# Placing the weight sums, the last run's row splits and the four-ahead row splits in a hybrid attention kernel

## The chip, the cores and the metric

The kernel runs on 1 core of one Trainium2 chip. The metric is the device time of one execution in microseconds (us), as the median of the runs given. The core has five engines with a queue each: TensorE (PE in the profile, with its weight loads as PEld), VectorE (DVE), ScalarE (ACT), GpSimd (POOL) and SyncE (SP), which here only issues DMAs. An engine takes its instructions in the order in which the program writes them to its queue; engines wait for one another, and for DMAs, through semaphores.

## The reference, cut to what matters

With DEPTH = 1 only the first layer runs, the one with the neighbourhood mixer. For x of 2048 tokens by 1024 columns, in float32:

```
h = rmsnorm(x, norm_0)
q, k, v, gate = split(h @ w_in_0, 4)               # 1024 x 4096
o = neighbourhood_attention(q, k, v, rpb_0)        # 16 heads of 64, 8 x 16 window on a 32 x 64 grid
x = x + (o * silu(gate)) @ w_out_0                 # 1024 x 1024
out = rmsnorm(x, norm_f)
```

Every matmul of the projections is done as three: an operand t is split into a high part h (ACT copies t to the rounding type fp32r) and a low part l = t - h (DVE), and the product is h·h + h·l + l·h. Part of the products are done by Strassen's scheme with seven block products in place of eight; for it sums and differences of blocks (called T1 to T4 on one side and S1 to S4 on the other) are formed and split too.

## The kernel before, in words

The program is written out by hand: Python code calls the engines in the order in which each queue is to work, and small closures are put into "slots" between groups of matmuls. Three parts matter here.

**Stage two** (`stage_two`) works on the second half of the tokens. First it forms the values v, as two groups of columns u = 0 and u = 1. `pair(u, ts, *do)` issues the 24 matmuls of each token tile in `ts` in four quarters (`values_of`, line L562) and calls `do[0]` to `do[3]` behind the quarters. Group 0 goes through four pairs of tiles, group 1 through eight single tiles 12, 13, 14, 15, 8, 9, 10, 11. In the slots stand:

- `lw`: loads of the weights of v by SP (L533); `w`: their splits, ACT L542 and DVE L545;
- `v`: the finished tile is taken from PSUM by ACT (L394) and stored by SP (L397);
- `block`, `t123`, `t4`, `form`, `t1`: sums and splits (ACT L520, DVE L521) of the token side for the seven products that follow;
- `out_rows(k)`: four loads of w_out rows by SP (L890), for k = 0 to 3; `out_sum(k, f)`: for T1, T3, T2, T4 in turn the difference of two of these rows on DVE (L897), its split (ACT L520 into `oh`, DVE L521 into `ol`) and two stores to DRAM by SP (L901), where the last stage fetches them;
- `ahead(i)`: loads, sums (DVE L427) and splits (ACT L420, DVE L421) of the weights for the seven products.

Then `run()` issues the seven products (L438) unit by unit in the order 1, 6, 2, 7, 5, 4, 3. Products 1 and 2 share a PSUM bank: `keep` (ACT L446) copies product 1 out before product 2 may be added to it, and `add` (DVE L451) does the like for 6 and 7.

**Attention** goes in 32 runs of (head pair, row block). `turns` transposes the probabilities on PE (L1136) and copies them from PSUM by ACT and DVE (L1112, three copies each); `values` multiplies them with v (L1158). Between them PE works on the `scores` (L1051) of the next run and on slices of other matmuls. Behind the last run there is no next one, so nothing lies between its transposes and its `values`.

**The output rows by seven products** (`rows_by_seven`) end the kernel: five pairs of output tiles, 35 products of 12 matmuls (L1439), of which the first 21 belong to pairs 0, 1 and 2 in an order written by hand (products 1 of the three pairs, products 2 of the three, and then mixed: places 16 to 20, counted from 0, are (1,3), (2,7), (2,5), (2,4), (2,3)), and 14 to pairs 3 and 4. `form_rows(m, P)` splits the operand of product P of pair m (ACT L1413, DVE L1414), `sum_rows` forms S1 to S4 (DVE L1420), `load_rows_of` fetches the blocks A11 to A22 (SP L1408). A table `todo` says behind which product each of these is issued. Behind a product, ACT or DVE take the result: L1444 for product 1, DVE L1449 and a sum on POOL (L1452, L1456) for 6 and 7, DVE L1236 (`add_rows`) for the rest; `finish` scales the finished rows (DVE L1279) some time later. Product 3 of a pair is added to the bank of product 5, so it waits until L1236 has read product 5.

The seven products' operands of the w_out side come back from DRAM through `land` (L1383). The splits of product 1 of pairs 0 to 2 stand ahead of `turns` of the last run, those of product 2 ahead of its `values`.

Of the kernel before, what the change touches and what calls it, by code (L numbers as in the profile page):

```python
# [32 lines left out]
PLAIN = 6  # L33
# [38 lines left out]
def build(ctx, tc, x, xr, xt, wg, rpb, last, w_out, n0, nf, masks, out):  # L72
# [728 lines left out]
    def stage_two():  # L801
        x12, x11, x21 = L2["x12"], L2["x11"], L2["x21"]
        x22 = [xp([128, 512], F32, "land") for _ in range(4)]
        sixth = sixths()
        for k in range(4):
            load_x(2, "x22", k, x22[k])
        slots = {"T2": [(mp, 512)] * 8,
                 "T3": [(sp, 512)] * 2 + sixth[:5] + [(lp, 512)],
                 "T4": [(vh, 512)] * 4 + [(mp, 512)] * 2 + [sixth[5], (qp, 512)]}

        def also(n, i):
            if n == 0:
                if i == 0:
                    load_ahead()
                    load_e(0, 0, xp)[0]()
                elif i == 1:
                    load_e(0, 0, xp)[1]()
                    load_masks()
                elif i == 2:
                    for f in load_e(order[1][0], 0, homes=accs):  # L820
                        f()
                if i in (1, 2, 3, 4):
                    consume(1)
                if i == 5:
                    consume(2)
                if i in (4, 5):
                    bias(0, 0, i - 4)
                if i == 3:
                    load_k(0, 0)()
                    load_q(0, 0)()  # L830

        ahead, run = seven_products(units_two, 2, X2, also)

        def pair(u, ts, *do):
            for b in range(4):
                values_of(X2, u, ts, (2 * b, 2 * b + 1))
                if b < len(do):
                    do[b]()

        def both(*fs):  # L840
            return lambda: [f() for f in fs]

        def block(f, x, *ks):
            def g():
                if f not in X2:
                    X2[f] = [(xs([128, 512], F32R, "h"), xs([128, 512], F32R, "l")) for _ in range(4)]
                for k in ks:
                    normed(f, 3, k, x[k])
# [12 lines left out]
        def t123(*ks):  # L861
            def g():
                for k in ks:
                    a, b, c = x11[k], x12[k], x22[k]
                    nc.vector.tensor_tensor(c, c, b, OP.subtract)
                    nc.vector.tensor_tensor(b, b, a, OP.subtract)
                    nc.vector.tensor_tensor(a, a, c, OP.add)
            return g

        def t4(*ks):  # L870
            def g():
                for k in ks:
# [12 lines left out]

        def out_rows(k):
            def g():
                for q, (r_, c_) in quarters.items():
                    OW[q] = kp([128, 960], F32, "ow")[:, :512] if r_ else ep([128, 512], F32, "ow")
                    nc.sync.dma_start(OW[q], w_out[(4 * r_ + k) * 128:(4 * r_ + k + 1) * 128, c_ * 512:c_ * 512 + 512])  # L890
            return g

        def out_sum(k, f):
            def g():
                a, b = {"T1": ("B12", "B11"), "T3": ("B22", "B12"), "T2": ("B22", "B11"), "T4": ("B21", "B22")}[f]
                o = OW[{"T1": "B11", "T3": "B12", "T2": "B22", "T4": "B21"}[f]]
                nc.vector.tensor_tensor(o, OW[a], OW[b], OP.subtract)  # L897
                h, l = ev([128, 512], F32R, "oh"), ev([128, 512], F32R, "ol")
                split_to(h, l, o, None)
                for i, s in enumerate((h, l)):  # L900
                    store(("ow", f, k, i), 5, lambda i=i, s=s: nc.sync.dma_start(wod[f][:, k, i], s.bitcast(F32)))  # L901
            return g

        def t1(*ks):
            def g():
                for k in ks:
                    split_to(*X2["B12"][k], x12[k], None)
                X2["T1"] = X2["B12"]
            return g

        pair(0, (8, 9), both(w(0, 3), lambda: spread_rstd(3)), both(lw(1, 0), block("B12", x12, 0, 1)),
             both(block("B12", x12, 2, 3), out_rows(0)), block("B22", x22, 0, 1))
        pair(0, (10, 11), both(v(0, 8, 9), block("B22", x22, 2, 3)), t123(0), t123(1), both(lw(1, 1), out_sum(0, "T1")))
        pair(0, (12, 13), both(v(0, 10, 11), out_sum(0, "T3")), t123(2), t123(3), both(t4(0, 1, 2, 3), lw(1, 2)))
        pair(0, (14, 15), both(v(0, 12, 13), w(1, 0), out_sum(0, "T2")), both(w(1, 1), lw(1, 3)), both(w(1, 2), out_sum(0, "T4")),
             both(w(1, 3), out_rows(1)))
        pair(1, (12,), v(0, 14, 15), form("T2", x11, 0), form("T2", x11, 1), out_sum(1, "T1"))
        pair(1, (13,), both(v(1, 12), form("T2", x11, 2)), form("T2", x11, 3), out_sum(1, "T3"), out_sum(1, "T2"))
        pair(1, (14,), both(v(1, 13), form("T3", x22, 0)), form("T3", x22, 1), out_sum(1, "T4"), out_rows(2))
        pair(1, (15,), both(v(1, 14), lambda: ahead(-9, -1)), form("T3", x22, 2), form("T3", x22, 3), out_sum(2, "T1"))  # L920
        pair(1, (8,), both(v(1, 15), lambda: ahead(-8, -1)), both(t1(0), out_sum(2, "T3")), t1(1), both(lambda: ahead(-7, -1), out_sum(2, "T2")))
        pair(1, (9,), both(v(1, 8), t1(2)), both(t1(3), out_sum(2, "T4")), both(lambda: ahead(-6, -1), out_rows(3)), form("T4", x21, 0))
        pair(1, (10,), both(v(1, 9), form("T4", x21, 1)), form("T4", x21, 2), both(form("T4", x21, 3), out_sum(3, "T1")), out_sum(3, "T3"))
        pair(1, (11,), both(v(1, 10), lambda: ahead(-5)), both(lambda: ahead(-4), out_sum(3, "T2")), both(lambda: ahead(-3), lambda: ahead(-2)),
             both(lambda: ahead(-1), v(1, 11), out_sum(3, "T4")))
        for k in range(4):
            hh[k, 2], hl[k, 2] = X2["B11"][k]
            hh[k, 3], hl[k, 3] = X2["B12"][k]
            hh[4 + k, 2], hl[4 + k, 2] = X2["B21"][k]
            hh[4 + k, 3], hl[4 + k, 3] = X2["B22"][k]  # L930
        run()
# [535 lines left out]
    def rows_by_seven():  # L1467
# [8 lines left out]
        def on(i, f, *a):  # L1476
            todo.setdefault(i, []).append((f, a))
# [11 lines left out]
            on(i, load_rest_of, m, j, k)  # L1489
        for m in range(E, len(PAIRS)):  # L1490
            s = seq.index((m, 1))
            for d, f in ((-7, "A21"), (-7, "A22"), (-6, "A11"), (-4, "A12")):
                on(s + d, load_rows_of, m, f)
            for d, f in ((-4, "S1"), (-4, "S2"), (-2, "S3"), (-1, "S4")):
                on(s + d, sum_rows, m, f)
            for d, j, k in ((-2, 0, 1), (-2, 0, 0), (-1, 1, 0), (0, 1, 1)):
                on(s + d, load_rest_of, m, j, k)
        for i, s in enumerate(seq):
            if i >= 2 * E:
                on(i - (LEAD if i < seq.index((E, 1)) else 3), form_rows, *s)  # L1500
        for f in ("A21", "A22"):
            load_rows_of(1, f, vh)
        for m in range(E):
            load_rest_of(m, 0, 0)
        land_T4()
        for i, (m, P) in enumerate(seq):
            rows_product(m, P)
            for d in sorted(todo):
# [77 lines left out]
    for m in range(cycles + 1):  # L1586
# [41 lines left out]
        if m == cycles:  # L1628
# [79 lines left out]
```

## Time and profile before

| | |
|---|---|
| times of the runs | 1059.3 us median of 3 (1059.07 to 1060.69) |
| the profiled execution's own time | 1060.0 us |
| its span, first to last instruction | 1058.2 us |
| mean granted TensorE clock | 0.995 |
| HBM traffic | 145.24 MB read, 58.72 MB written |
| slices of the span with PE at 9 tenths or more | 38 of 40 |

The profiled execution is one more run of the same program. A timeline row gives the start and the length of an instruction, its engine, its line and what it writes and reads, and in square brackets how long the engine had been idle before it and what ended that. The length of a matmul (0.39 us for 512 columns) is longer than the distance at which two can follow each other, since they overlap in the array. A row of SP is the issue of a DMA, not the transfer.

### The profile page before, as it was taken

The page shows a single profiled execution, that of the slowest core. Times are in us where ns is not written, and L with a number is a line of the kernel's source. Part 1 is how long each engine was busy: PE and PEld are TensorE (multiplying, and loading weights), DVE is VectorE, ACT ScalarE, POOL GpSimd, SP SyncE. Part 2 cuts the span into 40 slices and gives each one's busy share as a digit, 9 for nine tenths or more (in the row PEclk, how much of TensorE's full clock was granted, in tenths as well). Part 3 has the DMA queues.
Part 4 walks back from the last instruction along what each step waited for, and adds up shares of the span by engine and source line. Part 5 has one row for each costly group of instructions (what it writes and reads, how often), then busy time and mean ns, then how long its engine had stood idle before and what let it go on. Part 6 is the DMA issues. An engine that isn't in the chain of part 4 may idle for free.

```text
span 1058.2 us, 20319 instructions
## 1 busy us (share of the span) xinstructions
PE 1040.5 (98%) x7256; PEld 850.9 (80%) x7256; DVE 743.7 (70%) x1601; ACT 557.9 (53%) x1305; POOL 279.2 (26%) x357
## 2 busy tenths in 40 slices
PE   9999999999999999999999999999999999989997
PEld 6888888887888877888888788888888788878876
DVE  5376657778897857655554766677687797776986
ACT  7545323344344344332333477778888777663433
POOL 0000231322311000000000476755656424221331
PEclk9999999999999999999999999999999999999999
DMA  9633544443636587533244777788877599898452
GB/s 313 224 100 102 143 149 125 130 149 107 185 126 201 158 264 252 163 108 110 98 142 143 223 245 223 229 230 288 250 237 235 170 298 316 253 370 313 137 171 80
DMA packets 133213, 205.30 MB, mean 194 GB/s; under 512 B 12216, under 2 KB 56504, under 8 KB 133112
## 3 DMA queue, kind: packets, MB, share of 16 engines
q1 hardware_dynamic: 132680, 203.61, 60.6%
q8 instruction: 57, 0.93, 0.4%
q14 instruction: 44, 0.36, 0.1%
q10 hardware_dynamic: 432, 0.40, 0.1%
HBM read 145.24 MB, written 58.72 MB: 193 GB/s over the span
## 4 chain that ended last, share of the span: by engine, by line
PE 55%; DMA 2%; DVE 1%; ACT 1%; issue 1%; SPq 0%; DVEq 0%; ACTq 0%
PE pp L438 16%; PE py L1439 9%; PE s L1051 8%; PE o L1158 7%; PE ph L1136 4%; PE pp L384 2%; PE pp L386 2%; PE pp L382 2%; PE po L1360 2%; PE po L1362 2%; PE po L1364 2%; DMA t<-wodT 1%; DMA raw<-ogd 1%; DMA em<-in_last_dram 0%; DVE x L1059 0%
## 5 line engine op out<-in xcount | busy, mean ns | idle before, releaser
L438 PE MATMUL pp<-h,f 128*128 128x512 f32 x672 | 217.8, 389 | 2.8 <-ACT p L446 2.8
L1065 ACT ACTIVATE x<-x,st 128x360 f32<-128x360 f32 (+5 forms) x256 | 151.2, 592 | 24.7 <-DVE st L1059 24.7
L438 PEld LDWEIGHTS pp<-h,f 128*128 128x128 f32 x672 | 126.0, 188 | 29.5 <-ACT p L446 3.2
L438 PE MATMUL pp<-t,f 128*128 128x512 f32 x558 | 141.8, 389 | 0.1
L1079 POOL TENSOR_SCALAR x<-x,st 128x480 f32<-128x480 f32 (+5 forms) x192 | 114.4, 613 | 94.0 <-DVE st L1070 91.8
L438 PE MATMUL pp<-l,f 128*128 128x512 f32 x336 | 130.7, 389 | 0.0
L458 POOL TENSOR_TENSOR tmp<-tmp,rb 128x512 f32<-128x512 f32 x36 | 58.4, 1622 | 270.7 <-DVE tmp L456 235.3
L1059 DVE CUSTOM_DVE_ANT_0 x<-s,em 128x360 f32<-128x360 f32 (+5 forms) x256 | 123.0, 535 | 0.4 <-PE s L1051 0.4
L438 PEld LDWEIGHTS pp<-t,f 128*128 128x128 f32 x558 | 104.6, 188 | 22.5 <-DVE u L451 0.9
L1019 POOL TENSOR_TENSOR em<-e,mk 128x264 f32<-128x264 f32 (+3 forms) x64 | 50.8, 825 | 265.3 <-PE pp L438 251.8
L421 DVE TENSOR_TENSOR f<-raw,f 128x512 fp32r<-128x512 f32 x105 | 76.5, 729 | 37.5 <-ACT f L420 37.5
L1158 PEld LDWEIGHTS o<-pta,vt 120*64 120x64 f32 (+2 forms) x1792 | 82.7, 140 | 16.6 <-DVE st L1059 13.6
L1051 PE MATMUL s<-kt,q 64*128 64x480 f32 (+5 forms) x512 | 95.4, 487 | 0.1
L562 PE MATMUL pv<-wh,h 128*128 128x512 f32 x256 | 89.3, 394 | 2.0 <-ACT wh L542 2.0
L1158 PE MATMUL o<-pta,vt 120*64 120x128 f32 (+5 forms) x1792 | 87.4, 256 | 2.7 <-ACT pta L1112 2.4
L562 PE MATMUL pv<-wl,h 128*128 128x512 f32 x256 | 89.0, 393 | 0.3 <-DVE wl L545 0.3
L562 PE MATMUL pv<-wh,l 128*128 128x512 f32 x256 | 88.6, 391 | 0.0
L1051 PEld LDWEIGHTS s<-kt,q 64*128 64x128 f32 x512 | 64.7, 186 | 16.5 <-DVE pta L1112 2.3
L420 ACT ACTIVATE f<-raw 128x512 fp32r<-128x512 f32 x105 | 63.7, 624 | 26.2 <-PE pp L438 10.4
L1112 DVE COPY pta<-ph 120x512 f32<-120x512 f32 (+5 forms) x96 | 56.9, 639 | 23.9 <-PE ph L1136 23.7
L438 PEld LDWEIGHTS pp<-l,f 128*128 128x128 f32 x336 | 63.1, 188 | 13.1
L1112 ACT ACTIVATE pta<-ph 120x512 f32<-120x512 f32 (+5 forms) x96 | 49.5, 556 | 34.0 <-PE ph L1136 33.3
(186 smaller groups left out, 1861.4 us busy)
## 6 DMA issues: line engine op xcount, KB each, us to landing
raw<-in_wg_dram SPq DMA_DIRECT2D x124, 256.0 KB, 4.7
row<-in_xr_dram SPq DMA_DIRECT2D x32, 256.0 KB, 4.5
vd<-v SPq DMA_DIRECT2D x32, 256.0 KB, 3.0
sgd<-sg SPq DMA_DIRECT2D x32, 256.0 KB, 2.4
q<-qd SPq DMA_DIRECT2D x32, 256.0 KB, 5.6
sgt<-sgd SPq DMA_DIRECT2D x32, 256.0 KB, 6.3
xr<-in_x_dram SPq DMA_DIRECT2D x32, 256.0 KB, 5.2
ogd<-og SPq DMA_DIRECT2D x32, 256.0 KB, 4.0
```

Of the source, the lines that this page charges most:

```text
L420: nc.scalar.activation(t[:, 0], src, AF.Copy)
L421: nc.vector.tensor_tensor(t[:, 1], src, t[:, 0].bitcast(F32), OP.subtract)
L438: nc.tensor.matmul(B[n, P], t[:, int(m == 2), c], x[k][int(m == 1)], start=P in (1, 6, 5) and k == 0 and m == 0, stop=k == 3 and m == 2, s ...
L458: nc.gpsimd.tensor_tensor(tmp, tmp, rb[c], OP.mult)
L562: nc.tensor.matmul(ps[t], a[:, o], b, start=k == 0 and m == 0, stop=k == NK - 1 and m == 2)
L1051: nc.tensor.matmul(pst[s], qt[a, qs], kt[a, :r1 - r0, c0:c1].rearrange("p r (s c) -> p s r c", c=8), start=True, stop=True)
L1059: nc.vector.tensor_tensor_reduce(X[i, C][s], pst[s], EM[p, ROW_TYPE[T], COL_TYPE[C], s], -1.0, 1e38, OP.add, OP.min, st[:, o:o + 1])
L1065: nc.scalar.activation(X[i, C][s], X[i, C][s], AF.Exp, bias=st[:, o:o + 1], scale=-1.0, accum_out=st[:, 4 + o:5 + o])
L1079: nc.gpsimd.tensor_scalar(X[i, C][s], X[i, C][s], st[:, o:o + 1], 1.0, op0=OP.mult, op1=OP.mult)
L1112: (nc.vector.tensor_copy if h else lambda o, i_: nc.scalar.activation(o, i_, AF.Copy))(t[:k, h, b * 512:b * 512 + w], banks_[b, h][:k, :w])
L1158: nc.tensor.matmul(to.rearrange("d (h q) -> d h q", q=64) if nq > 64 else to, vt[:k, strip, s * 64:s * 64 + 64], t[:k, h, at:at + 64] if n ...
L1439: nc.tensor.matmul(B[m, P], t[:, a, c], b, start=P in (1, 6, 5) and k == 0 and i == 0, stop=k == 3 and i == 2, skip_group_check=True)
```

## The change

Three edits, all of them to the order in which things are issued; no operation is added or taken away.

1. In `stage_two`, `out_sum` is cut in two: `out_sum` does only the difference, `out_split` the split and the stores. In the list of pairs a sum now stands one slot ahead of its split, and the loads `out_rows(1)`, `(2)`, `(3)` and the sums are moved to other slots. For k = 3 the last split stands in tile 10's last slot, and tile 11's slots hold none.
2. The splits of product 1 of pairs 0 to 2 are issued behind the last run's `turns`, and those of product 2 behind its `values`, at the head of `rows_by_seven`.
3. In `rows_by_seven` the splits of pairs 3 and 4 are issued four products ahead in place of three, their S1, S3 and loads one to three products earlier.

```diff
                 o = OW[{"T1": "B11", "T3": "B12", "T2": "B22", "T4": "B21"}[f]]
                 nc.vector.tensor_tensor(o, OW[a], OW[b], OP.subtract)
+            return g
+
+        def out_split(k, f):
+            def g():
+                o = OW[{"T1": "B11", "T3": "B12", "T2": "B22", "T4": "B21"}[f]]
                 h, l = ev([128, 512], F32R, "oh"), ev([128, 512], F32R, "ol")
                 split_to(h, l, o, None)
...
+        def o(k, *fs):
+            return [(out_sum if f[0] == "+" else out_split)(k, "T" + f[-1]) for f in fs]
+
...
-        pair(0, (10, 11), both(v(0, 8, 9), block("B22", x22, 2, 3)), t123(0), t123(1), both(lw(1, 1), out_sum(0, "T1")))
-        pair(0, (12, 13), both(v(0, 10, 11), out_sum(0, "T3")), t123(2), t123(3), both(t4(0, 1, 2, 3), lw(1, 2)))
-        pair(0, (14, 15), both(v(0, 12, 13), w(1, 0), out_sum(0, "T2")), both(w(1, 1), lw(1, 3)), both(w(1, 2), out_sum(0, "T4")),
-             both(w(1, 3), out_rows(1)))
...
-        pair(1, (10,), both(v(1, 9), form("T4", x21, 1)), form("T4", x21, 2), both(form("T4", x21, 3), out_sum(3, "T1")), out_sum(3, "T3"))
-        pair(1, (11,), both(v(1, 10), lambda: ahead(-5)), both(lambda: ahead(-4), out_sum(3, "T2")), both(lambda: ahead(-3), lambda: ahead(-2)),
-             both(lambda: ahead(-1), v(1, 11), out_sum(3, "T4")))
+        pair(0, (10, 11), both(v(0, 8, 9), block("B22", x22, 2, 3)), t123(0), t123(1), both(lw(1, 1), *o(0, "+1")))
+        pair(0, (12, 13), both(v(0, 10, 11), *o(0, "=1", "+3")), both(t123(2), *o(0, "=3", "+2")), both(t123(3), *o(0, "=2", "+4")),
+             both(t4(0, 1, 2, 3), lw(1, 2), *o(0, "=4")))
+        pair(0, (14, 15), both(v(0, 12, 13), w(1, 0), out_rows(1)), both(w(1, 1), lw(1, 3)), w(1, 2), w(1, 3))
...
+        pair(1, (10,), both(v(1, 9), form("T4", x21, 1), *o(3, "+2")), both(form("T4", x21, 2), *o(3, "=2")),
+             both(form("T4", x21, 3), *o(3, "+4")), both(*o(3, "=4")))
+        pair(1, (11,), both(v(1, 10), lambda: ahead(-5)), lambda: ahead(-4), both(lambda: ahead(-3), lambda: ahead(-2)),
+             both(lambda: ahead(-1), v(1, 11)))
...
-            for d, f in ((-7, "A21"), (-7, "A22"), (-6, "A11"), (-4, "A12")):
+            for d, f in ((-9, "A21"), (-8, "A22"), (-7, "A11"), (-6, "A12")):
                 on(s + d, load_rows_of, m, f)
-            for d, f in ((-4, "S1"), (-4, "S2"), (-2, "S3"), (-1, "S4")):
+            for d, f in ((-5, "S1"), (-4, "S2"), (-3, "S3"), (-1, "S4")):
                 on(s + d, sum_rows, m, f)
...
-                on(i - (LEAD if i < seq.index((E, 1)) else 3), form_rows, *s)
+                on(i - LEAD, form_rows, *s)
...
         land_T4()
+        for m in range(E):
+            form_rows(m, 2)
...
-        if m == cycles:
-            for n in range(3 if PLAIN <= 6 else 2):
-                form_rows(n, 1)
         sums = next_sums(m) == m + 1
...
             land_T2()
-            for n in range(3 if PLAIN <= 6 else 2):
-                form_rows(n, 2)
+            for n in range(3):
+                form_rows(n, 1)
```

The slots of k = 1 and 2 in group 1 are moved in the same way. In the built order of each queue nothing outside these three places is moved.

More of the change, by code (lines that the diff above doesn't have):

```diff
@@ L915, in stage_two @@
-        pair(0, (14, 15), both(v(0, 12, 13), w(1, 0), out_sum(0, "T2")), both(w(1, 1), lw(1, 3)), both(w(1, 2), out_sum(0, "T4")),
-             both(w(1, 3), out_rows(1)))
[L917 to L920, printed above, removed]
@@ L921, in stage_two @@
-        pair(1, (8,), both(v(1, 15), lambda: ahead(-8, -1)), both(t1(0), out_sum(2, "T3")), t1(1), both(lambda: ahead(-7, -1), out_sum(2, "T2")))
-        pair(1, (9,), both(v(1, 8), t1(2)), both(t1(3), out_sum(2, "T4")), both(lambda: ahead(-6, -1), out_rows(3)), form("T4", x21, 0))
-        pair(1, (10,), both(v(1, 9), form("T4", x21, 1)), form("T4", x21, 2), both(form("T4", x21, 3), out_sum(3, "T1")), out_sum(3, "T3"))
-        pair(1, (11,), both(v(1, 10), lambda: ahead(-5)), both(lambda: ahead(-4), out_sum(3, "T2")), both(lambda: ahead(-3), lambda: ahead(-2)),
-             both(lambda: ahead(-1), v(1, 11), out_sum(3, "T4")))
+        pair(0, (10, 11), both(v(0, 8, 9), block("B22", x22, 2, 3)), t123(0), t123(1), both(lw(1, 1), *o(0, "+1")))
@@ new lines, in stage_two @@
+        pair(0, (12, 13), both(v(0, 10, 11), *o(0, "=1", "+3")), both(t123(2), *o(0, "=3", "+2")), both(t123(3), *o(0, "=2", "+4")),
+             both(t4(0, 1, 2, 3), lw(1, 2), *o(0, "=4")))
+        pair(0, (14, 15), both(v(0, 12, 13), w(1, 0), out_rows(1)), both(w(1, 1), lw(1, 3)), w(1, 2), w(1, 3))
+        pair(1, (12,), v(0, 14, 15), both(form("T2", x11, 0), *o(1, "+1")), both(form("T2", x11, 1), *o(1, "=1")), both(*o(1, "+3")))
+        pair(1, (13,), both(v(1, 12), form("T2", x11, 2), *o(1, "=3")), both(form("T2", x11, 3), *o(1, "+2")), both(*o(1, "=2", "+4")),
+             both(*o(1, "=4")))
@@ new lines, in stage_two @@
+        pair(1, (14,), both(v(1, 13), form("T3", x22, 0), out_rows(2)), form("T3", x22, 1), both(), both(*o(2, "+1")))
+        pair(1, (15,), both(v(1, 14), lambda: ahead(-9, -1), *o(2, "=1", "+3")), both(form("T3", x22, 2), *o(2, "=3")),
+             both(form("T3", x22, 3), *o(2, "+2")), both(*o(2, "=2", "+4")))
+        pair(1, (8,), both(v(1, 15), lambda: ahead(-8, -1), *o(2, "=4")), both(t1(0), out_rows(3)), t1(1), lambda: ahead(-7, -1))
+        pair(1, (9,), both(v(1, 8), t1(2), *o(3, "+1")), both(t1(3), *o(3, "=1")), both(lambda: ahead(-6, -1), *o(3, "+3")),
+             both(form("T4", x21, 0), *o(3, "=3")))
```

## The prediction, on record before the run

> **What bounds the kernel now.** I read the page, then the waits of PE, then each wait's place in the timelines.
>
> ```profile
> PE 1040.5 (98%) x7256; PEld 850.9 (80%) x7256; DVE 743.7 (70%) x1601; ACT 557.9 (53%) x1305; POOL 279.2 (26%) x357
> ...
> PE pp L438 <- ACT p L446: 2.8, 1, 2.8
> PE o L1158 <- ACT pta L1112: 2.4, 1, 2.4
> PE py L1439 <- DVE y L1236: 2.3, 1, 2.3
> PE pv L562 <- ACT wh L542: 2.0, 2, 1.2
> ```
>
> TensorE sets the end. The change touches none of its work, so it can gain only where PE waits, and the last four rows are nearly all of that outside the start. The three edits aim at them: edit 1 at the first and fourth (stage two), edit 2 at the second (last run), edit 3 at the third (output rows).
>
> **Edit 1, the end of stage two.**
>
> ```profile
> 421.86 0.69 DVE L897 TENSOR_TENSOR ow<-ow 128x512 f32<-128x512 f32 x1
> 422.63 0.63 ACT L520 ACTIVATE oh<-ow 128x512 fp32r<-128x512 f32 x1 [1.77 <-issue]
> 423.29 0.69 DVE L521 TENSOR_TENSOR ol<-ow,oh 128x512 fp32r<-128x512 f32 x1 [0.74 <-ACT oh L520]
> 423.17 0.58 ACT L446 ACTIVATE p<-pp 128x512 f32<-128x512 f32 x1
> 423.80 0.50 PE L438 MATMUL pp<-h,f 128*128 128x512 f32 x1 [2.75 <-ACT p L446]
> ...
> 423.80 166.41 PE pp L438 x732
> ```
>
> The last T4 sum stands behind DVE's other work; ACT waits 1.77 us for it with the copy of product 1 queued behind, and PE waits 2.75 us for that copy. (The last row is the chain's: matmuls follow each other by 166.41 / 732 = 0.227 us, a product of twelve takes 2.73.) In the changed queues no sum or split stands in tile 11's slots; ACT has only the six splits, the v copy, then L446. It is free when product 1 ends. **Term: -2.75.**
>
> What is late next is the first split of the run, which now stands behind all sixteen splits of sums.
>
> ```profile
> 394.19 0.69 DVE L897 TENSOR_TENSOR ow<-ow 128x512 f32<-128x512 f32 x1 [3.43 <-DMA ow<-in_w_out_dram]
> 389.55 1.91 SPq L890 DMA_DIRECT2D ow<-in_w_out_dram  x4
> ```
>
> A sum can follow its load by 394.19 - 389.55 = 4.6 us. A split's high part (head, oh) follows its sum by 0.77, its low part (tail, ol) the head by 0.66, and DVE does one such operation per 0.6 (rows above). I walked the new DVE queue with these steps from 375, when the last weights of v are split (rows below): T4's tail of k = 1 at 386; its store, which stands ahead in SP's queue, lets `out_rows(2)` go at 387; first sum at 391.6, T4's tail of k = 2 at 400.4, `out_rows(3)` at 400.8, first sum at 405, T4's tail of k = 3 at 414.4, and the run's first tail at 416.1. The run starts two products and the wait before 423.80, at 415.6; with what the next paragraph adds, and its third matmul the first to need the tail, PE asks for it at 416.9. **Term: +0.2**, between 0 and the whole 2.75 (the wait only changes place).
>
> **Edit 1, the weights of the last quarter.** Group 1's fourth weights are loaded late (`lw(1, 3)`).
>
> ```profile
> 353.43 0.69 DVE L897 TENSOR_TENSOR ow<-ow 128x512 f32<-128x512 f32 x1
> 371.09 0.69 DVE L521 TENSOR_TENSOR ol<-ow,oh 128x512 fp32r<-128x512 f32 x1 [0.75 <-ACT oh L520]
> 367.76 1.07 SPq L397 DMA_DIRECT2D vd<-v  x2
> 368.87 1.06 SPq L533 DMA_DIRECT2D raw<-in_wg_dram  x2
> 372.19 2.05 SPq L890 DMA_DIRECT2D ow<-in_w_out_dram  x4
> 373.87 1.17 ACT L542 ACTIVATE wh<-raw 128x512 fp32r<-128x512 f32 x2 [2.81 <-DMA raw<-in_wg_dram]
> 375.10 0.49 PE L562 MATMUL pv<-wh,h 128*128 128x512 f32 x1 [1.23 <-ACT wh L542]
> ```
>
> The loads leave SP at 368.87, behind T2's tail store, and land as ACT's row shows 5 us later; PE waits. In the changed SP queue they stand behind T4's tail store and the four `out_rows(1)` issues too. From the first sum at 353.43, DVE now does, with no idle round trips, three more sums, four tails, six t123 and four t4 operations, 17 of 0.6 plus 0.12 on six dependent ones and the 1.4 of the first head: T4's tail ends at 365.7, not 371.8. SP: store to 366.1, four loads of 2.0, two stores of 1.07: `lw(1, 3)` at 369.2, 0.3 later than now. Ahead of them 1.05 MB of `out_rows` is in flight: at the 406 GB/s that a row below shows 2.6 us, of which the issue itself covers 2.0. **Term: +0.3 + 0.6 = +0.9.** Bounds: -1.5 (both waits here vanish) to +2.9 (nothing of the 2.6 covered). The group's other weight tails end about 369.4 on DVE as now.
>
> **Edit 2, the last run.**
>
> ```profile
> 943.63 1.43 PE L1136 MATMUL ph<-ident,x 64*96 64x64 f32 x44
> 944.77 1.15 ACT L1413 ACTIVATE f<-raw 128x512 fp32r<-128x512 f32 x2 [0.62 <-DMA raw<-ogd]
> 946.64 1.74 DVE L1112 COPY pta<-ph 96x512 f32<-96x512 f32 x3
> 948.44 4.11 PE L1158 MATMUL o<-pta,vt 96*64 96x64 f32 x48 [0.36 <-DVE pta L1112]
> 952.48 0.80 PE L1439 MATMUL py<-woh,f 128*128 128x512 f32 x1
> 955.45 0.40 PE L1439 MATMUL py<-wol,f 128*128 128x512 f32 x1
> ...
> 921.44 1.43 PE L1136 MATMUL ph<-ident,x 64*96 64x64 f32 x44
> 922.13 1.59 ACT L1112 ACTIVATE pta<-ph 96x512 f32<-96x512 f32 x3 [0.49 <-PE ph L1136]
> 925.37 2.67 PE L1158 MATMUL o<-pta,vt 96*64 96x128 f32 x56
> ...
> 950.00:952.00 2.00, 2.00 (x28) 2.00 (x28) 0.31 (x1) 0.00 (x0) 0.00 (x0) 0.50 1.05 406
> 422.00:424.00 2.00, 0.20 (x1) 0.20 (x2) 1.24 (x2) 1.37 (x3) 0.00 (x0) 1.00 0.63 158
> ```
>
> Both copiers stand behind row splits that wait for a DMA. Moved behind the copies, these leave the copies as in the run at 922: ACT starts 0.7 behind the first transpose, 944.3; DVE too, ending 1.8 later, 946.15. The bulk of o then starts at 946.2 instead of 948.44. **Term: -2.24.**
>
> The windows' clock column falls to 0.50 in this place. 48 of o take 4.11 us here, where 56 take 2.67 in the run at 925, so 2.29 for 48: 1.82 lost. The seven py from 952.48 to 955.45 take 2.97, where seven at 0.227 take 1.59: 1.38 lost. With copies on time PE's stretch without dense matmuls is 943.6 to 946.2, 2.6 us with a few of o inside, instead of 3.8; the stall of 2.75 us before 423.80 has its clock at 1.00. So I take it that the clock stays. **Term: -3.2**, between 0 and that.
>
> The Trainium skill (TensorE: Matmul & The Clock Gate, "What's actually happening") says that the clock is halved after about one idle window of 3.4 us, free-running. The trace agrees: 3.8 us fell, 2.75 did not. By the free phase the same gap can meet a window otherwise, and the page's Part 4 ("PE-mode transpose") says that transposes don't count as busy in the same way: by that rule rival 1 is open.
>
> The moved splits must be ready in time: ACT is done with the copies at 945.9 and one square at 946.65, the first head then takes 0.5 and its tail follows at 947.4 to 948.1; product 1 starts at 948.4 and needs the tail at its third matmul. Products 2 start 8.2 later. Hidden; without that cover 0.7 would show.
>
> **Edit 3, the output rows.**
>
> ```profile
> 1005.32 0.68 DVE L1420 TENSOR_TENSOR s<-raw 128x512 f32<-128x512 f32 x1
> 1006.04 1.67 DVE L1420 TENSOR_TENSOR s<-s,raw 128x512 f32<-128x512 f32 x1
> 1007.63 2.44 DVE L1279 SCALAR_TENSOR_TENSOR y<-y,st,acc 128x512 f32<-128x512 f32 x2
> 1007.12 1.73 POOL L1456 TENSOR_TENSOR p<-p,xr 128x512 f32<-128x512 f32 x1
> 1010.82 0.47 PE L1439 MATMUL py<-woh,f 128*128 128x512 f32 x1 [2.28 <-DVE y L1236]
> ```
>
> Product 3 of pair 2 waits for the read of product 5. That product ended a product and the wait before 1010.82, at 1005.8; DVE reads it only behind the L1279 row, which ends at 1010.07. S1 of pair 3 moves up, ahead of u; but a split (product 1 of pair 3) comes in between u and the read instead. The number of operations there stays. DVE has little idle time before u, so u comes 0.35 later and POOL, which starts on u's result, too; DVE's all-SBUF operations that meet a POOL sum are stretched (1.67 for 0.68), and L1279 again must wait for its end. The read comes at 1010.5. **Term: +0.45**, between -2.28 (wait gone) and +1.7 (one more POOL sum met). The loads are issued by SP earlier than needed; the other splits lie in idle DVE time.
>
> **The sum:** -2.75 + 0.2 + 0.9 - 2.24 - 3.2 + 0.45 = -6.6. The profiled execution took 1060.0 us, so 1053.4; the median of the runs is 0.7 lower: **1052.7**.
>
> **Rivals**, in the median's scale.
>
> 1. The clock falls in the last run all the same: + 3.2, **1055.9**. For it: transposes and a wait still meet there. Against: the gap is shorter than one that kept its clock.
> 2. The wait before product 2 takes place at product 1: its first split comes 2.75 late, for it stands behind sixteen splits and two loads that I walked with an error of some 2 us: 2.55 more, **1055.3**.
> 3. The lead won in the last run is lost among the output rows, since DMA sets their pace:
>
> ```profile
> 960.00:970.00 10.00, 10.00 (x46) 8.28 (x45) 6.47 (x10) 4.24 (x10) 0.00 (x0) 1.00 1.06 387
> 954.86 0.32 SPq L1383 DMA_DIRECT2D wol<-wodT  x1
> ...
> wol<-wodT SPq DMA_DIRECT2D x4, 256.0 KB, 6.0
> ...
> 961.21 0.69 DVE L1420 TENSOR_TENSOR s<-raw 128x512 f32<-128x512 f32 x1 [2.96 <-DMA raw<-ogd]
> ```
>
>    The DMA share (the column before the last) is full to 970. T2's last tile is issued at 954.86 and lands in the 6.0 of its group, 960.9; the product that needs it would start six products behind 948.4, at 964.8; DVE's S1 of pair 1 waits for a load to 961.21, which leaves DVE some 3 us behind PE; the idle time that it has in these windows (6.5 busy of 10) lets it catch up by 968. If it isn't, 2.24 + 3.2 come back: **1058.1**.
> 4. Slower: the weights of the last quarter. Should T4's tail stay at 371.8 (ACT and DVE still waiting on each other), then SP has its store to 371.8, four loads and two stores to 374.9, and the weights come 6.0 + 0.6 later than now, 5.7 beyond my term. PE then idles 8 us, longer than the 3.8 that halved the clock, and pays 3.2 more at half speed: **1061.6**. It decides against the change from 3.4 us beyond my term on (6.6 less 3.2), if the clock falls with it. Against it: the sums need no head in between.
>
> **How the numbers follow.** Forecast 0.52, rivals 0.18, 0.14, 0.10, 0.06. A measurement of this kernel tells 0.2%, 2.1 us, from no change. The forecast and rivals 1 and 2 lie below 1057.2: 0.84 faster; rival 3 lies within 0.2%: 0.09; rival 4 with its neighbourhood: 0.07 slower. The range goes from 1049.5 (weights' wait partly gone, third wait smaller: 3 us better) to 1057.5, which takes in rivals 1 and 2 with their spread.
>
> **What would show it.** No PE wait for L446 near 421; ACT's L542 near 374 still waiting for `raw`, its SP issue behind L890; copies L1112 of the last run starting within 1 us of the transposes, with a clock of 1.00 behind; PE's wait for L1236 near 1003 still 2 to 3 us. The prediction is wrong if the clock there falls, if a wait for L420 or L421 stands at the first product of the run, or if PE waits between the rows' seventh and fifteenth product.

## The result, and the profile after

The changed kernel took **1055.4 us** (median of 6, 1053.9 to 1057.0) against 1059.4 (median of 6, 1058.4 to 1060.7): ratio 0.9961, 95% interval 0.9948 to 0.9975. Forecast were 1052.7, in a range from 1049.5 to 1057.5. The profiled execution of the changed kernel took 1056.7; its span is 1054.9, where that of before was 1058.2. One execution of the experiments (of the kernel with the scaling behind the read) took 1890 us at a clock of 0.777 and stands in none of the numbers below. Lines behind `stage_two` stand 11 or 12 higher than before: L1112 is now L1124, L1136 L1148, L1158 L1170, L1236 L1248, L1279 L1291, L1413 L1425, L1420 L1432, L1439 L1451, L1449 L1461. The stores of the sums, L901, are now L906, and L446 is the same.

TensorE's waits in the changed kernel (total, times, longest):

```profile
PE pv L562 <- ACT wh L542: 4.4, 2, 3.7
PE py L1451 <- DVE y L1248: 2.2, 1, 2.2
...
PE py L1451 <- DVE u L1461: 0.4, 1, 0.4
...
PE py L1451 <- ACT f L1425: 0.3, 1, 0.3
```

Of the four large waits of before, that for L446 (2.8) is gone, that for ACT's `pta` (2.4) is gone, that for the read of product 5 is as it was, and that for the last quarter's weights has grown. Its row holds two waits, as it did before: one of 0.8 at the very start of the kernel (PE at 5.5), which is the same in both, and one here, 1.23 before and 3.67 now. With the wait for L545 right behind it, the starts of PE's matmuls give 1.9 before and 4.4 now. Two small ones among the output rows are new (u L1461, f L1425).

**Where L446 was waited for.** Timeline of the changed kernel, ACT, DVE and PE:

```profile
418.74 0.62 ACT L420 ACTIVATE f<-raw 128x512 fp32r<-128x512 f32 x1
...
423.44 0.59 ACT L446 ACTIVATE p<-pp 128x512 f32<-128x512 f32 x1
...
419.39 0.69 DVE L421 TENSOR_TENSOR f<-raw,f 128x512 fp32r<-128x512 f32 x1 [0.31 <-ACT f L420]
...
419.68 0.39 PE L438 MATMUL pp<-h,f 128*128 128x512 f32 x1
...
420.14 0.73 PE L438 MATMUL pp<-h,f 128*128 128x512 f32 x2
```

The run's first split head is ready at 419.36, the run starts at 419.68, and the first tail ends at 420.08, just ahead of the third matmul at 420.14. L446 runs at 423.44 with no idle time before it, and PE has no gap from there on. Nothing is late at product 1, but with less than 0.1 us to spare.

**The last run.** The same view, PE and ACT:

```profile
944.88 1.43 PE L1148 MATMUL ph<-ident,x 64*96 64x64 f32 x44
...
947.45 2.23 PE L1170 MATMUL o<-pta,vt 96*64 96x64 f32 x48 [0.40 <-DVE pta L1124]
949.61 0.50 PE L1451 MATMUL py<-woh,f 128*128 128x512 f32 x1
...
945.57 1.59 ACT L1124 ACTIVATE pta<-ph 96x512 f32<-96x512 f32 x3 [3.04 <-PE ph L1148]
```

ACT's copies start 0.7 behind the transposes, the 48 of o take 2.23 (4.11 before), and from the transposes to the first row product go 949.61 - 944.88 = 4.73 us, where before had 952.48 - 943.63 = 8.85.

**The last quarter's weights.** SP, ACT and PE of the changed kernel:

```profile
366.07 0.33 SPq L906 DMA_DIRECT2D wodT<-ol  x1
366.45 1.94 SPq L890 DMA_DIRECT2D ow<-in_w_out_dram  x4
368.49 0.93 SPq L397 DMA_DIRECT2D vd<-v  x2
369.61 1.37 SPq L533 DMA_DIRECT2D raw<-in_wg_dram  x2
...
376.75 1.15 ACT L542 ACTIVATE wh<-raw 128x512 fp32r<-128x512 f32 x2 [8.27 <-DMA raw<-in_wg_dram]
...
377.95 0.51 PE L562 MATMUL pv<-wh,h 128*128 128x512 f32 x1 [3.67 <-ACT wh L542]
```

The chain that ended last goes through that transfer:

```profile
369.61 7.05 DMA raw<-in_wg_dram
```

And the windows (last three columns: clock, DMA share, GB/s) show the DMA engines full while the weights wait, and the clock halved behind:

```profile
366.00:368.00 2.00, 2.00 (x11) 1.65 (x10) 2.00 (x5) 1.49 (x4) 0.00 (x0) 1.00 1.00 363
368.00:370.00 2.00, 2.00 (x10) 1.68 (x9) 1.65 (x3) 0.48 (x1) 0.00 (x0) 1.00 1.01 289
370.00:372.00 2.00, 2.00 (x10) 1.66 (x9) 0.00 (x0) 0.00 (x0) 0.00 (x0) 1.00 0.91 248
...
378.00:380.00 2.00, 1.70 (x5) 1.15 (x6) 1.28 (x3) 1.90 (x4) 0.00 (x0) 0.81 0.36 110
380.00:382.00 2.00, 2.00 (x7) 1.54 (x6) 1.85 (x4) 1.21 (x3) 0.00 (x0) 0.50 0.51 152
382.00:384.00 2.00, 2.00 (x9) 1.67 (x8) 1.90 (x4) 1.58 (x3) 0.00 (x0) 0.83 0.68 262
```

With a share of 0.91 to 1.01 they move 363, 289, 248 GB/s, not 406. The low rate is not the whole of the 7.05: in windows of half a microsecond the share is 0.39 from 375.0 and below 0.1 from 375.5, and ACT starts at 376.75, so for about 1 us the DMA engines are nearly idle and the weights' split has not started. A clock of c in a window of 2 us means 4 x (1 - c) us at half speed: 0.76 + 2.00 + 0.68 = 3.4 us, of which half, 1.7, is lost. The weights leave SP at 369.61 and are used 7.1 later; before it was 368.87 and 5.0 later.

**The output rows.** DVE and PE:

```profile
999.78 0.67 DVE L1432 TENSOR_TENSOR s<-raw 128x512 f32<-128x512 f32 x1
...
1001.72 0.68 DVE L1461 TENSOR_TENSOR u<-py,p 128x512 f32<-128x512 f32 x1
...
1002.91 1.79 DVE L1426 TENSOR_TENSOR f<-raw,f 128x512 fp32r<-128x512 f32 x1
1004.62 2.43 DVE L1291 SCALAR_TENSOR_TENSOR y<-y,st,acc 128x512 f32<-128x512 f32 x2
1006.98 0.68 DVE L1248 TENSOR_TENSOR y<-py,u 128x512 f32<-128x512 f32 x1
...
1002.54 0.47 PE L1451 MATMUL py<-t,f 128*128 128x512 f32 x1 [0.42 <-DVE u L1461]
1007.80 0.47 PE L1451 MATMUL py<-woh,f 128*128 128x512 f32 x1 [2.25 <-DVE y L1248]
```

The order is as forecast: S1 (999.78) is ahead of u, a split stands between u and the read, then the scaling, then the read. PE's wait is 2.25 where it was 2.28. DVE has hardly any idle time here, as the windows show (behind the length of the window come the busy times of PE, PEld, DVE, ACT and POOL):

```profile
995.00:1000.00 5.00, 4.70 (x22) 3.60 (x21) 4.70 (x9) 1.36 (x4) 1.67 (x1) 1.00 0.38 148
1000.00:1005.00 5.00, 4.58 (x21) 3.47 (x20) 4.70 (x9) 1.97 (x5) 2.47 (x2) 1.00 0.61 219
1005.00:1010.00 5.00, 2.75 (x13) 1.97 (x12) 5.00 (x7) 1.76 (x4) 0.84 (x1) 1.00 0.46 149
```

From the first row product to the span's end go 1054.9 - 949.61 = 105.3 us; before it was 1058.2 - 952.48 = 105.7, of which 1.4 were the matmuls at half clock. So the rows got 0.9 longer, about what the two small waits for f and u take.

### The profile page after: what moved, and what is told of

The parts are those of the page before. It is cut to its first block, busy times and chain, and to the rows that moved or that the text cites. A ratio compares the mean times of both kernels' runs of the same rounds, so it can differ in the third digit from the quotient of the medians.

```text
span 1054.9 us, 20328 instructions
## 1 busy us (share of the span) xinstructions
PE 1039.0 (98%) x7256; PEld 850.1 (81%) x7256; DVE 743.2 (70%) x1601; ACT 558.4 (53%) x1305; POOL 278.1 (26%) x357
## 4 chain that ended last, share of the span: by engine, by line
PE 89%; DVE 7%; issue 1%; ACT 1%; DMA 1%; POOL 0%; ACTq 0%; DVEq 0%
PE pp L438 36%; PE pv L562 12%; PE s L1063 8%; PE o L1170 8%; PE py L1451 7%; PE ph L1148 4%; PE pp L384 2%; PE po L1372 2%; PE po L1374 2%; PE pp L386 2%; PE pp L382 2%; PE po L1376 2%; DMA raw<-in_wg_dram 1%; DVE l L521 1%; DVE y L1291 1%
## 5 line engine op out<-in xcount | busy, mean ns | idle before, releaser
L1170 PEld LDWEIGHTS o<-pta,vt 120*64 120x64 f32 (+2 forms) x1792 | 80.9, 137 | 14.4 <-DVE st L1071 13.6
L1170 PE MATMUL o<-pta,vt 120*64 120x128 f32 (+5 forms) x1792 | 85.5, 253 | 0.5 <-DVE pta L1124 0.4
L420 ACT ACTIVATE f<-raw 128x512 fp32r<-128x512 f32 x105 | 63.8, 624 | 27.8 <-PE pp L438 12.5
L1124 DVE COPY pta<-ph 120x512 f32<-120x512 f32 (+5 forms) x96 | 56.9, 639 | 23.9 <-PE ph L1148 23.8
L1124 ACT ACTIVATE pta<-ph 120x512 f32<-120x512 f32 (+5 forms) x96 | 49.7, 557 | 37.1 <-PE ph L1148 36.4
```

Source lines behind the costliest of these rows:

```text
L420: nc.scalar.activation(t[:, 0], src, AF.Copy)
L1124: (nc.vector.tensor_copy if h else lambda o, i_: nc.scalar.activation(o, i_, AF.Copy))(t[:k, h, b * 512:b * 512 + w], banks_[b, h][:k, :w])
L1170: nc.tensor.matmul(to.rearrange("d (h q) -> d h q", q=64) if nq > 64 else to, vt[:k, strip, s * 64:s * 64 + 64], t[:k, h, at:at + 64] if n ...
```

## The experiments

Each kernel was timed beside the kernel before in five rounds. Ratios are to before, with the 95% interval.

| kernel | median us | ratio |
|---|---|---|
| changed | 1055.4 | 0.9961 (0.9948 to 0.9975) |
| edit 1 alone | 1059.3 | 0.9998 (0.9989 to 1.0007) |
| edit 2 alone | 1056.8 | 0.9974 (0.9964 to 0.9984) |
| edit 3 alone | 1060.4 | 1.0010 (1.0000 to 1.0021) |
| edits 1 and 2 | 1056.4 | 0.9964 (0.9952 to 0.9976) |
| changed, weights ahead of out_rows | 1053.8 | 0.9950 (0.9937 to 0.9964) |
| changed, out_rows in the last slot | 1052.2 | 0.9933 (0.9920 to 0.9946) |
| the same, scaling behind the read | 1050.8 | 0.9924 (0.9909 to 0.9939) |
| changed, weights in buffers of their own | 1049.1 | 0.9895 (0.9878 to 0.9912) |
| the same, last split and scaling moved too | 1047.3 | 0.9884 (0.9868 to 0.9900) |
| the same, additions on DVE | 1048.1 | 0.9885 (0.9869 to 0.9901) |
| last split and scaling moved, five ahead | 1048.6 | 0.9904 (0.9885 to 0.9924) |
| the same, scaling at 48 | 1050.1 | 0.9915 (0.9898 to 0.9931) |

The theory after the first comparison of traces: edits 1 and 2 do what was forecast at their two waits, and the gain that is missing went into one transfer, the last quarter's weights behind `out_rows(1)`. The rivals: it went into the output rows, or another engine is as late as the weights.

**Edit 1 alone.** The kernel before with the new lists of `stage_two`.

> The kernel before with edit 1 alone (stage two). Theory: the wait for L446 goes (-2.9), the wait for the last quarter's weights grows by 2.5 and the clock falls behind it (+1.5): sum +1.1 to 0, so 1059.4 to 1060.5; the last run keeps its wait and its fall of the clock. The forecast's own terms for this edit (-2.75 + 0.2 + 0.9) would give -1.65, 1057.7. Rival (edit 1 made the whole gain): 1055.4.

Measured: no change at all. Waits of that kernel:

```profile
PE pv L562 <- ACT wh L542: 3.4, 1, 3.4
PE py L1451 <- DVE y L1248: 2.3, 1, 2.3
PE o L1170 <- ACT pta L1124: 2.1, 1, 2.1
```

The wait for L446 is gone and one of 3.4 for the weights stands in the list instead; its windows at 374 to 382 show the clock at 0.54, 0.50, 0.50, 0.75. What edit 1 takes away at 421 it pays at 375: the first theory, not the forecast's -1.65, nor the rival that it made the whole gain.

**Edit 2 alone.** The kernel before with the first row splits behind the last run's copies.

> The kernel before with edit 2 alone (first row splits behind the last run's copies). Theory: wait 2.24 and clock 3.2 go, the last run ends 5.4 to 5.5 earlier, 1053.9; clock 1.00 throughout 943 to 956. Rival (the lead is lost among the output rows): the gain at the last run is there but some of it comes back as waits between 960 and 1030: 1056 to 1058. Rival (without edit 1's shift of time the free-running clock window falls otherwise): clock falls, 1057.

Measured: -2.5, less than half of 5.4. The last run itself did what was expected, 948.00 - 943.28 = 4.72 from the transposes to the first row product, at a clock of 1.00. The rest was lost elsewhere. Waits, then windows of the output rows:

```profile
PE pp L438 <- ACT p L446: 2.7, 1, 2.7
PE py L1439 <- DVE y L1236: 2.3, 1, 2.3
PE py L1439 <- ACT f L1413: 1.9, 2, 1.5
```

```profile
1008.00:1010.00 2.00, 2.00 (x7) 1.57 (x7) 2.00 (x5) 1.60 (x5) 0.00 (x0) 0.63 0.99 250
1010.00:1012.00 2.00, 2.00 (x7) 1.54 (x6) 0.48 (x4) 0.72 (x2) 0.00 (x0) 0.52 0.88 293
```

Two waits for row splits, 1.9 together, are new: PE comes earlier than ACT and DVE can follow. And in this execution the old wait of 2.3 for the read of product 5 was followed by 3.4 us at half clock; in before and in the changed kernel it was not. The same happened behind the wait for L446 (clock 0.86, 0.50, 0.79 in the windows from 420 to 426), which edit 2 does not touch. Each of the two costs up to 1.7. The profiled execution is the slowest of the twelve; the four with a mean clock of 0.998 or more took 1054.5 to 1055.7, close to the expected 1053.9, the other eight 1056.4 to 1058.6. So forecast and rival 3 both hold a part: the last run gains 5.4 nearly whole, and it goes again in part to the clock behind other waits and in part to the order of DVE's and ACT's work among the rows, not to a transfer, as rival 3 had it.

**Edit 3 alone.** The kernel before with the new offsets (loads one or two products earlier, S1 and S3 one) and a lead of four.

> The kernel before with edit 3 alone (loads, sums and splits of later output rows earlier). Theory (the new small waits of 0.46 and 0.58 among the rows come from edit 3's order): wait for L1236 stays 2.3 to 2.5, about +0.5 to +1, 1060 to 1060.4. Rival (those waits come from PE's lead of edit 2 and edit 3 does nothing): 1059.4, no change. Forecast's term: +0.45.

Measured: 1.1 slower, with an interval that just reaches no change. Alone it gains nothing. Its profile does not show why: of the two small waits only one of 0.16 for u is there, and the clock fell behind the wait for L446 (0.84, 0.50, 0.81 from 422 to 428), where edit 3 changes nothing.

**Edits 1 and 2 without edit 3.**

> The changed kernel without edit 3 (loads, sums and splits of the later output rows as before). Alone, edit 1 gave 0, edit 2 -2.5, edit 3 +1.1, while all three gave -4.0. Theory (edit 3 pays only when PE arrives early among the output rows, which edit 2 brings about: its earlier splits take away the 1.6 and 0.6 that PE waited for f in edit 2 alone): edits 1 and 2 give -2.5, 1056.7, with waits for f of about 2 together. Rival (the edits add up, and the sum of the single runs is only noise): all three less edit 3's +1.1, 1054.3, or without any part of edit 3 1055.4.

Measured: -3.3 by medians, where all three have -4.0; the intervals overlap. The wait for f is 1.2 here and 0.3 with edit 3, in the direction of the theory (which had about 2), but the times do not tell the two apart, and the expected 1056.7 and 1055.4 lie either side of the 1056.4 within its spread. What edit 3 is worth stays open: alone it cost 1.1, beside the other two it gained 0.7 by medians and 0.3 by ratios, and none of this is clear of noise.

**The weights ahead of the loads.** The changed kernel with

```
-pair(0, (14, 15), both(v(0, 12, 13), w(1, 0), out_rows(1)), both(w(1, 1), lw(1, 3)), w(1, 2), w(1, 3))
+pair(0, (14, 15), both(v(0, 12, 13), w(1, 0)), both(w(1, 1), lw(1, 3), out_rows(1)), w(1, 2), w(1, 3))
```

> The changed kernel with out_rows(1) issued behind lw(1, 3) instead of two slots ahead of it. Theory (the weights' transfer stands in the DMA queues behind 1 MB of out_rows): the two loads leave SP near 366.5, land by 372, PE's two waits for L542 (3.84 and 0.58) fall to 0 to 1 us together, and the clock stays 1.00 at 378 to 382, so 4.4 + 1.5 less: about 1049.5 (before less 9 to 10). Rival (DVE's order, the splits of sums ahead of the weights' own splits, is what holds PE): the loads land earlier but ACT's wh or DVE's wl comes no earlier, a wait of 2 to 4 us stays, 1053 to 1055.

Measured: 1.6 below the changed kernel's 1055.4, within the intervals, and not 6. The time lies in the rival's range, but not for its reason: ACT waits for the DMA, not for DVE. SP, ACT and PE of that kernel:

```profile
365.31 1.38 SPq L533 DMA_DIRECT2D raw<-in_wg_dram  x2
366.74 2.38 SPq L890 DMA_DIRECT2D ow<-in_w_out_dram  x4
...
371.32 0.63 ACT L542 ACTIVATE wh<-raw 128x512 fp32r<-128x512 f32 x1 [5.03 <-DMA raw<-in_wg_dram]
373.34 0.63 ACT L542 ACTIVATE wh<-raw 128x512 fp32r<-128x512 f32 x1 [1.39 <-DMA raw<-in_wg_dram]
...
374.02 0.50 PE L562 MATMUL pv<-wh,h 128*128 128x512 f32 x1 [1.98 <-ACT wh L542]
```

The first half is used 6.0 behind its issue, the second only at 373.34, and PE waits 1.98 for it. The windows behind (0.93, 0.50, 0.72 from 374 to 380) make 3.4 us at half clock out of it. The place in the queue was a part of the cause, not the whole. An earlier place is not to be had as the program stands: `raw` has six buffers, enough for three quarters, and the fourth may start only when the split of the first has freed two.

**out_rows in the last slot.** As before had it, the weights in the second slot as above.

> The changed kernel with out_rows(1) in the last slot of tiles 14 and 15, as the kernel before had it, but lw(1, 3) still in the second slot. In the run with out_rows right behind lw(1, 3) the weights were issued at 365.31 and used by ACT at 371.32, 6.0 later; PE still waited 2.1. Theory (transfers issued behind the weights share the DMA engines with them and stretch their landing): ACT uses them within 5.0 to 5.3 of the issue, PE's waits there fall below 1 together, the clock stays 1.00, about 3 to 4 less than that run's 1053.75: 1050 to 1051. Rival (the latency is set by what was issued ahead, the stores of v and of the sums): still 6.0, wait of 2, clock falls or not by its phase: 1053 to 1054.

Measured: 1052.2, with

```profile
371.59 1.28 ACT L542 ACTIVATE wh<-raw 128x512 fp32r<-128x512 f32 x2 [5.18 <-DMA raw<-in_wg_dram]
```

6.2 behind the issue at 365.39. The test didn't separate the theories, since SP had nothing to wait for between the slots: `out_rows(1)` left at 366.88, right behind the weights, as in the kernel above. Only the second half of the weights landed sooner here, PE waited 0.8, and the clock stayed. With equal orders on SP, the wait was 2.0 in one profile and 0.8 in the other, with the half clock behind the longer alone. A wait of 1.3 for f L420 at the run's first product came up, which is rival 2 in small.

**The weights in buffers of their own.** The changed kernel with these two loads into `rbp`, which is idle there, and one pair of tiles earlier:

```
-return lambda: [load_v0(u, a, b) for b in bs for a in range(2)]
+return lambda: [load_v0(u, a, b, rbp([128, 512], F32, "raw") if (u, b) == (1, 3) else None) for b in bs for a in range(2)]
...
-both(t123(2), *o(0, "=3", "+2"))
+both(t123(2), lw(1, 3), *o(0, "=3", "+2"))
...
-both(w(1, 1), lw(1, 3)), w(1, 2), w(1, 3))
+w(1, 1), w(1, 2), w(1, 3))
```

> The changed kernel with the last quarter's weights lw(1, 3) loaded into two buffers of their own (rbp, idle there) from the second slot of tiles 12 and 13, so that they neither wait for a free raw buffer nor stand behind out_rows(1) and the stores of v; nothing else is moved. Theory (this one transfer is the mis-sized term, a wait of 4.4 in the changed kernel and a half clock behind it of 1.5 to 1.6): waits for L542 and L545 at 371 to 375 gone, clock 1.00 at 376 to 384, and since the run is then reached some 6 earlier, a wait for f L420 of 1.5 to 3 at its first product, as the kernel with the loads last showed 1.5; 0.5 more among the output rows. 1055.4 - 4.4 - 1.5 + 2 + 0.5 = 1052. Rival (another engine is as late as the weights): a wait of over 2 at the same place with another name, 1054 to 1055.

Measured: **1049.1**, 6.3 below the changed kernel and 10.5 below before. Waits and a window:

```profile
PE py L1451 <- DVE y L1248: 2.3, 1, 2.3
...
PE pv L562 <- ACT wh L542: 0.6, 1, 0.6
```

```profile
372.00:376.00 4.00, 4.00 (x19) 3.34 (x18) 3.28 (x5) 1.85 (x5) 0.00 (x0) 1.00 0.99 310
```

The 0.6 for L542 lies at the very start of the kernel. The weights now leave SP at 357.15, and at 372 to 376 PE is busy throughout, though the DMA engines are full behind `out_rows(1)` (366.12) and the stores of v. The wait that was feared at the run's first product did not come. So the one transfer held 4.4 + 1.7 of the changed kernel: the theory, and against the rival that another engine is as late. Of the 6.3, a place ahead of `out_rows(1)` alone gave 1.6 (above); the rest came with the 8 us earlier start that the buffers allow.

**The scaling behind the read.** The kernel with out_rows in the last slot and

```
-store(("y", n), 12 if n == tiles - 2 else 24, scale)
+store(("y", n), 12 if n == tiles - 2 else 36, scale)
```

> As the kernel with the loads last, and the output rows' scaling (L1291) due 36 instead of 24 matmuls behind its root, which puts it behind DVE's read of product 5 of pair 2 instead of ahead of it. Theory (DVE's queue order sets the waits among the output rows): the waits for y L1248 (2.4) and for ACT's f L1425 (0.5 to 1.1, whose head stands behind a root that waits for DVE behind a scaling) go, 2.5 to 3.5 less than the kernel with the loads last. Rival (DVE is full there, so the wait moves to the next operation that the scaling now delays): within 1 of the kernel with the loads last.

Measured: 1050.8, or 1.4 less, 0.9 by the ratios, and the intervals overlap: nearer to the rival, with the theory's 2.5 to 3.5 not reached. Of its waits

```profile
PE py L1451 <- DVE f L1426: 1.8, 1, 1.8
PE pv L562 <- ACT wh L542: 1.8, 1, 1.8
PE py L1451 <- DVE u L1461: 1.6, 1, 1.6
```

that for y L1248 is gone, and u L1461 has 1.6 instead of 0.4. The second row is the weights' again. The first is rival 3's mechanism after all: DVE stands idle for a load, and PE gets the split that follows at 964.18:

```profile
962.04 0.69 DVE L1432 TENSOR_TENSOR s<-raw 128x512 f32<-128x512 f32 x1 [4.84 <-DMA raw<-ogd]
```

Behind both of these waits of 1.8 the clock fell, for 3.4 us each. In the changed kernel DVE waits 4.12 for the same load, but there the split ends at 963.8 and the matmul that needs it starts at 966.5, so the load is 2.7 us from being the next limit.

**Last split and scaling moved.** The kernel with the weights in buffers of their own, the scaling as above, and the last split of sums behind the run's first two splits:

```
-both(form("T4", x21, 3), *o(3, "+4")), both(*o(3, "=4")))
+both(form("T4", x21, 3), *o(3, "+4")), both())
...
-lambda: ahead(-4), both(lambda: ahead(-3), lambda: ahead(-2))
+both(lambda: ahead(-4), *o(3, "=4")), both(lambda: ahead(-3), lambda: ahead(-2))
```

> The kernel with the weights early, the last split of sums (T4 of k = 3) put behind the run's first two splits, and the scaling of the output rows due 36 matmuls behind its root. Theory: no wait over 1 at 371, at 412 and for y L1248; one of 1.5 to 2 for u L1461 near 1000 stays, as with the scaling behind the read. 3 to 4 below the kernel with the weights early: 1048 to 1049. Rival (DVE is full both before 412 and before 1000, so each move only shifts its wait): 1051 or more.

Measured: **1047.3**, the lowest median of all; it beats both kernels (ratio 0.9884 to before). From the kernel without these two moves the intervals don't separate it, so the theory's gain is not shown. Its waits for u (1.7) and f (1.6) stay.

**Additions on DVE instead of POOL.** L1464 and L1468 by `nc.vector`.

> As the kernel with all moves, and the three additions of x to u and p1 of the output rows (L1464 twice, L1468) on DVE instead of POOL. POOL's additions of 1.6 to 1.75 each stretch DVE's operations beside them (0.68 to 1.7 and 1.41 to 2.44 in the traces so far); on DVE they take 0.6. Theory (a POOL addition costs DVE 1.0 while it holds it up, more than the 0.6 of doing it): the wait for u near 1000 shrinks by 0.5 to 1.5, 0.5 to 1 below the kernel with all moves. Rival (POOL's work is hidden mostly and DVE gets three more operations per pair): up to 1 slower.

Measured: 1048.1, not to be told from 1047.3. The stretching is gone: with POOL idle, the split at 998.30 takes 0.68 and the scaling at 990.57 takes 1.41, where the kernel with all moves has 1.79 and 2.45. That is 2.2 us less for DVE, and the three additions take 1.8, at 0.6 each.

**Splits five products ahead, and the scaling at 48.** `LEAD if s[0] < 2 else 5`; then 48 for the scaling and 60 for its store.

> As the kernel with all moves, and the splits of the output rows from pair 2 on placed five products ahead instead of four. Theory (the wait of PE for ACT's f L1425 at 988.9 there, 0.96, is a head queued on ACT behind a root that waits for DVE: 988.74 st, then 988.85 f; one product more ahead puts it before that root): that wait goes, 0.5 to 1 less, 1046.5; the wait of 1.9 for u L1461 stays. Rival (DVE is full there and gets the tails earlier): the wait for u grows by as much, 1047.3.

> As the kernel with splits five products ahead, and the scaling of the output rows due 48 matmuls behind its root (its store to DRAM 60). Theory (the scaling that now stands ahead of u L1461 is what PE's 1.9 at 995.4 waits for): that wait falls below 0.7, 1 to 1.5 less, 1045 to 1045.5. Rival (DVE is full from 983 to 1005, so it only moves on): a wait of 1 to 2 for y L1248 at product 5 or 4 of pair 2 comes back, 1046.5 to 1047.3.

Measured: 1048.6 and 1050.1, both no gain; of the second

```profile
PE py L1451 <- DVE y L1248: 2.3, 1, 2.3
PE py L1451 <- ACT f L1425: 1.3, 1, 1.3
```

the wait for y is back at 2.3, as its rival said, and that for f did not go in either. A likely reason, which no run tests by itself, is DVE's load: it is busy 4.7 to 5.0 of 5 us in the windows above, and 4.2 to 4.8 from 985 to 1005 in the second of these kernels, so that a move mostly names another product that waits.

## Why the prediction was right in sign and range, and 2.7 too low

By its own steps, profiled spans (-3.3) against its sum (-6.6):

- **Wait for L446, -2.75: right** (2.9 by the starts of PE's matmuls). What was named as late next, the first split, was walked to 416.1 for its tail against a run at 415.6; the tail ended 0.4 behind the run's start, 0.06 before it was needed, and **+0.2 was 0**, by a hair.
- **Weights of the last quarter, +0.9: the mis-sized term.** The mechanism, and its first half, were right: T4's tail store was forecast for 366.1 at the latest and runs from 366.07 to 366.40; the weights leave SP at 369.61, where 369.2 was forecast. The step that failed is "at the 406 GB/s" and "2.6 us, of which the issue itself covers 2.0": the transfer took 7.05 instead of 5.6. The rate was taken from the last run; in this place the engines, as full, moved 248 to 363 GB/s, with stores of sums and v between the loads. That the stores lower the rate is not tested. By an estimate, 1.05 MB at the mean of 300 GB/s take 3.5 us, which gives 0.9 of the missing 1.45; the rest stays open. PE's two waits here, for L542 and L545, grew by 2.5 (upper bound given: +2.9).
- **The clock there, not in the sum at all: +1.7.** Rival 4 had the half clock at the weights, but only behind a wait of 8 us, since the sum took a gap's length as the rule: "the stall of 2.75 us before 423.80 has its clock at 1.00". A wait of 3.7 was enough, and that the rule itself doesn't hold is shown by other kernels (below), where 1.8 and 2.0 were enough.
- **Last run, -2.24 - 3.2: right**, 8.85 to 4.73 and the matmuls at half clock behind it gone, 5.5 together. The clock stayed at 1.00 there in all eleven kernels with edit 2, and fell in the three without it, behind waits of 2.0 to 2.4. The reason given, a gap shorter than one that kept its clock, is not what made it so, since waits of 1.8 and 2.0 lost it elsewhere.
- **Output rows, +0.45: somewhat low.** The wait for the read did not change (2.28 to 2.25); two small waits ahead of it came, and the stretch grew by 0.9. Rival 3 was right that the rows take back a part of the lead, and wrong in its cause in this kernel: no transfer reaches PE there, the waits are for DVE and ACT. In later kernels one does (the scaling behind the read).

Put together: -2.9 + 2.5 + 1.7 - 5.5 + 0.9 = -3.3, as measured between the two profiles. That edit 1 alone gave nothing, and that the weights in their own buffers gave 6.3, bear out the second and third terms. The time by itself would have misled: 1055.4 is what rival 2 (1055.3) and nearly what rival 1 (1055.9) forecast, and neither happened, for there is no wait at the run's first product and the clock in the last run is 1.00.

## What to carry to other kernels

When a load is moved ahead in a queue that other loads share, price the load that now stands behind it by its landing in the worst row the trace has, not by bandwidth alone, and look first whether an idle buffer lets it start early: that was worth more here than the whole change. Price each wait of TensorE with the chance of a half clock behind it. And in a stretch where one engine is nearly full, expect a move of its work to rename the wait: none of the five kernels that tried it among the output rows gained clear of noise.

## What the runs showed of the hardware

**The length of a wait doesn't tell whether the half clock follows.** In the fourteen profiles each stretch at half clock behind these waits lasts 3.4 or 6.8 us, so costs up to 1.7 or 3.4: the wait of 2.7 for L446 kept its clock in before and lost it in two of the kernels that still have it (edits 2 and 3 alone: 0.50 around 422 to 426); the wait of 2.3 among the rows lost it with edit 1 alone and edit 2 alone, and kept it in eight others; the weights' wait for L542 lost it in the five kernels where it was 1.8 or more (3.7, 3.5, 3.4, 2.0, 1.8) and kept it where it was 1.6 or less. The Trainium skill (TensorE: Matmul & The Clock Gate, "What's actually happening") has a free-running window of 3.4 us and a fall after about one idle window. The length of the stretches agrees; that a whole idle window is needed does not, since 2.0 us of waiting did (1.98 in the kernel with the weights ahead of the loads). One profile therefore doesn't tell what a wait costs: one and the same program, edit 2 alone, had mean clocks of 0.995 to 1.000 in its twelve runs, and the times went with them. Some of the spread of before (1056.6 to 1062.7 over its runs beside the experiments) is likely of this kind: its 13 runs at a clock of 0.993 have a mean of 1060.1, its 13 at 0.996 one of 1058.7.

**Landing times.** The same two loads of 256 KB were used 5.0 us after their issue behind three stores, and 7.1 behind four loads and three stores. With one and the same order on SP, they were used together at 6.2 in one profile, and 2.0 apart in another.
